# Where the Norms' second halves and block 2's gates stand in a two-block trunk kernel

## The chip, the cores and the metric

The kernel runs on one core of a Trainium2 chip. The metric is the device time of one execution in microseconds, the median of several runs. The core has five engines with an instruction queue each: TensorE (PE), VectorE (DVE), ScalarE (ACT), GpSimd (POOL) and SyncE (SP), which here issues the DMAs.

## The reference

Two blocks of two layers each are computed over 512 latent tokens (`x`) and 256 context tokens (`ctx`), all with 1024 features in float32. Every layer of block 1 is a mixer (layer 0 an mLSTM, layer 1 a windowed attention), then a feed-forward part; each has a Norm ahead of it, which scales a token by the reciprocal of its root mean square and then scales and shifts its features:

```python
u = _modulate(_rms_norm(h, norm_mix[i]), mod_l[0], mod_l[1])
h = h + mod_l[2] * y                      # y: the mixer's output product
h = h + mod_l[5] * _sq_relu_mlp(_modulate(_rms_norm(h, norm_ffn[i]), mod_l[3], mod_l[4]), ...)
```

A layer of block 2 has three branches over the same input, a gate for each, one output product and a LayerNorm:

```python
mixed = jnp.einsum('gts,bnsgc->bntgc', w_s, vn) + b_s.T[None, None, :, :, None]     # in sgu
m = (jax.nn.sigmoid(ga) * (ya @ p['w_br_attn']) + jax.nn.sigmoid(gg) * (yg @ p['w_br_gla'])
     + jax.nn.sigmoid(gs) * (ys @ p['w_br_sgu']))
x_new = layer_norm(DEEPNORM_ALPHA * x + gate[:, None, :] * (m @ p['w_out']), p['post_g'], p['post_b'])
```

`ya` comes from an attention, `yg` from a gated linear attention (gla, a scan over chunks of 64 tokens) and `ys` from a spatial gating unit (sgu): `mixed` is its spatial product, within chunks of 128 tokens. `ga`, `gg` and `gs` are 1024 features each of a product of the layer's input with weights. The last layer of a block needs the latent tokens alone.

## The kernel before, in words

Features lie on the 128 partitions, tokens along the free axis. A product in float32 accuracy is made of three: an operand is split in a high and a low part (`whi`, `wlo` of the weights, `uhl`, `ull` of latent and `uhc`, `ulc` of context activations), and high-high, high-low and low-high are summed in a PSUM bank. A block of 128 output features over a segment so takes 8 x 3 = 24 matmuls. Segments are `LAT` (512 latent tokens), `CTX` (256 context tokens) and `HALVES` (the latent tokens in two halves, `H0` and `H1`). Two banks (`acc`) go round among the products, in some stages more (`accx`); a bank is free again when DVE or ACT has read it.

`sweep` (L397) runs a product over blocks and segments. At the end of a stage its last `nt` blocks (`tail`; 3, with LayerNorm 4 or 5) are taken segment by segment, so that the next Norm can be formed for the first segment while the second's products run. This is in the hands of a `Norm` object (L1894; `LayerNorm`, L1935, in block 2) with four calls: `add` accumulates squares of the residual in DVE and ACT (`nac`, `nal`, in LayerNorm `nsl`, `nsc` too), `stat` sums them over the partitions by matmuls with `onesd` (`colsum`) and takes the power -1/2 on POOL (`rs`, in LayerNorm `rv`), `spread` brings the result to all partitions by a matmul with the identity into the bank `ns`, and `make` forms the 8 blocks of `uh`, `ul` with it: a DVE product `sc`, an ACT modulation `uh`, a DVE or POOL difference `ul`. There are six stage ends with a Norm: A the mLSTM's output product, B the first ffn's, C the windowed attention's, D the second ffn's, E and F the output products of block 2's two layers. F is the end of the kernel.

In `b_layer` (L1731), `gla` (L1421) runs in pools of its own and calls `fill` for work that PE does between the steps of its scan. A step works in levels (`gqt`, `gkq` on DVE in two buffers each, then the small products `P` and `sm`). `fill` issues the gates (24 blocks of 128 features, L1640, a bank is freed by ACT's tanh and the result stored by a DMA to `th`) and `sgu` (L1585). The spatial products of sgu stand in four groups; each group and segment takes a bank, which DVE frees with the product `sc<-acc,vecs,st`, and POOL multiplies the result with `us`. In layer 0 a gate covers `LAT` and `CTX`, in layer 1 `LAT` alone. After gla, `merge` loads the branches and the gates again.

The order within an engine is not the order of the code: a scheduler with a model of time chooses among the instructions whose inputs it takes for ready, and the order of the code gives the priority. Each engine then works its list in order. Names in listings carry numbers: `acc_21963` is one use of a bank.

Of the kernel before, what the change touches and what calls it, by code (L numbers as in the profile page):

```python
# [239 lines left out]
class Net:  # L240
# [156 lines left out]
    def sweep(self, items, x, segs, use, kt=8, head=None, tail=None, nm=None, nt=3):  # L397

        n = len(items)

        def group(js, segs, nm=None):
            w = [self.ws(*items[j], kt) for j in js]
            for i, s in enumerate(segs):
                for j, wj in zip(js, w):
                    use(j, s, self.fm(wj, [x(s)], kt)[0])
                    self.step()
                    if nm and i and j == js[0]:
                        nm.spread(segs[i - 1])  # L410
                if nm:
                    nm.stat(s)
                    if i:
                        nm.make(segs[i - 1])
            if nm:
                nm.spread(segs[-1])
                nm.make(segs[-1])

        a, b = 3 if head else 0, n - nt if tail else n
        if head:  # L420
            group(range(a), head)
        for j in range(a, b):
            group([j], segs)
        if tail:
            with self.weights("wt", nt) if nt > 3 else contextlib.nullcontext():
                group(range(b, n), tail, nm)
# [1155 lines left out]
                y = slice(t * P + 32 * b, t * P + 32 * b + 32)  # L1582
                self.mm(pS[t // 2][32 * b:32 * b + 32, t % 2, lev, :], k[:, y], q[:, y])

    def sgu(self, u, l, ph, d, between):  # L1585
        nc = self.nc
        full = l == 0
        us = self.t(ph, [P, 4, T if full else TL], "us")
        segs = [LAT, CTX][:1 + full]
        wT, bs, t2 = [self.t(ph, [P, 512], n) for n in ("swT", "sbs", "st2")]  # L1590
        nc.sync.dma_start(out=wT, in_=self.ins["swT"][l])
        nc.sync.dma_start(out=bs, in_=self.ins["sgu_b"][l].partition_broadcast(P))
        ps = self.acc()
        self.mm(ps, self.ones, wT)
        for g in range(4):
            x = slice(g * P, (g + 1) * P)
            self.stt(t2[:, x], ps[:, x], self.vec("sgu_ln_b_2", 1, l * 4 + g), bs[:, x], MULT, ADD)

        def items(n):
            return [((n, l, i), c) for i in range(2) for c in range(2)]  # L1600

        def up(f, s, ps):
            x = us[:, f, self.cols(s)]
            self.stt(x, x, 0.5, ps, MULT, MULT)

        self.sweep(items("b_sg"), lambda s: self.part(u, s), segs,
                   lambda f, s, ps: self.silu2(ps, us[:, f, self.cols(s)]))
        self.sweep(items("b_su"), lambda s: self.part(u, s), segs, up)
        chunks = range(6 if full else 4)
        sv = self.t(ph, [P, len(chunks), 512], "sv")  # L1610
        for i in range(2):
            w = self.wt(("b_sv", l, i))
            for c in chunks:
                ps = self.acc(256)
                self.tmm(ps, self.uchunk(u, c), w)
                (self.act if c % 2 else nc.vector.tensor_copy)(sv[:, c, i * 256:(i + 1) * 256], ps)
        for c in chunks:
            b6 = self.t(ph, [P, 6], "sb6", bufs=2)
            mv = self.t(ph, [P, 2], "smv", bufs=2)
            nc.vector.bn_stats(b6, sv[:, c, :])  # L1620
            nc.vector.bn_aggr(mv, b6)
            self.ts(mv[:, 1:2], mv[:, 1:2], EPS, ADD)
            self.tt(mv[:, 1:2], mv[:, 1:2], self.nhalf[:, 0:1], ALU.pow, eng=nc.gpsimd)
            self.ts(sv[:, c, :], sv[:, c, :], mv[:, 0:1], SUB, mv[:, 1:2], MULT)
        between()
        for g in range(4):
            x = slice(g * P, (g + 1) * P)
            for s in segs:
                y = self.cols(s)
                nt, c0 = s.n // P, y.start // P  # L1630
                ps = self.acc(s.n).rearrange("p (t x) -> p t x", x=P)
                for t in range(nt):
                    self.mm(ps[:, t, :], sv[:, c0 + t, x], wT[:, x])
                m = self.scr(s.n)
                self.stt(m.rearrange("p (t x) -> p t x", x=P), ps, self.vec("sgu_ln_g_2", 1, l * 4 + g),
                         t2[:, x].unsqueeze(1).to_broadcast([P, nt, P]), MULT, ADD)
                self.tt(us[:, g, y], m, us[:, g, y], MULT, eng=nc.gpsimd)
                nc.sync.dma_start(out=d["ys"][:, g, y], in_=us[:, g, y])

    def gates(self, u, l, d, items):  # L1640

# [89 lines left out]
    def b_layer(self, u, l, x_src, norm, x_dst, xd):  # L1731

        nc = self.nc
        segs = [s for s in ("l", "c") if s == "l" or l == 0]
        ntok = {"l": TL, "c": TC}
        tail = [LAT, CTX] if l == 0 else HALVES
        d = {n: self.t(xd, sh, f"{n}{l}") for n, sh in
             (("ya", [P, 4, T]), ("yg", [P, 4, T]), ("ys", [P, 4, T]), ("gg", [P, 4, T]), ("gv", [P, 6, 512]), ("gqk", [4, P, T]),  # L1740
              ("th", [24, P, T]))}
        g0 = 3 + l

        def fill():
            self.gla_in(u, l, d)
            self.gates(u, l, d, range(0, g0))

        self.b_attn(u, l, d["ya"], fill)
        if self.dbg_fn:
            self.dbg(f"ya{l}", d["ya"])  # L1750

        def fill():
            a, b = ((6, 9), (8, 10))[l]
            self.gates(u, l, d, range(g0, a))
            with self.pool("sg") as ph:
                self.sgu(u, l, ph, d, lambda: self.gates(u, l, d, range(a, b)))
            self.gates(u, l, d, range(b, 24))

        self.gla(u, l, d, fill)
        if self.dbg_fn:  # L1760
            self.dbg(f"yg{l}", d["yg"])
            self.dbg(f"ys{l}", d["ys"])
        def residual(ph):

            z = {s: self.t(ph, [P, KC, ntok[s]], "z" + s) for s in segs}
            rs, w = self.t(ph, [P, TL], "rs"), self.t(ph, [P, 2, 8], "wb")
            for s, r in norm[0]:
                ps = self.acc(s.n)
                self.spread(ps, r)
                self.act(rs[:, s.o:s.o + s.n], ps)  # L1770
            for i, v in enumerate(norm[1:]):
                if v is not None:
                    self.ts(w[:, i], v, ALPHA, MULT)
            for s in segs:
                nc.sync.dma_start(out=z[s], in_=x_src[s])
                for c in range(KC):
                    x = z[s][:, c, :]
                    if s == "c":
                        self.act(x, x, scale=ALPHA)
                        continue  # L1780
                    self.tt(x, x, rs, MULT, eng=nc.gpsimd)
                    if norm[2] is None:
                        self.act(x, x, scale=w[:, 0, c:c + 1])
                    else:
                        self.act(x, x, AF.Identity, scale=w[:, 0, c:c + 1], bias=w[:, 1, c:c + 1])
            return z

        with contextlib.ExitStack() as es:
            y, z = {}, None
            if l:  # L1790
                ph = es.enter_context(self.pool("ln", side="right"))
            with self.pool("mg") as pm, self.banks(6, 0):
                if l:
                    z = residual(ph)
                self.merge(pm, l, d, y)
            if not l:
                ph = es.enter_context(self.pool("ln", side="right"))
            with self.banks(2, 4):

                z = z or residual(ph)  # L1800
                gh = self.t(ph, [P, 8, 2], "gh")[:, :, :len(segs)]
                self.ts(gh, self.mod2[l][:, 16:24, :len(segs)], 0.5, MULT)
                un = {} if l == 0 else None
                nm = LayerNorm(self, ph, z, l, un, x_dst)
                self.proj_res([("b_wo", l, i) for i in range(4)], y, z, {s: gh[:, :, "lc".index(s)] for s in segs},
                              [LAT, CTX][:len(segs)], tail, nm, nt=5 - l)
        return un, [(s, nm.r[s][1]) for s in tail if s.kind == "l"]
# [222 lines left out]
```

## Time and profile before

| | |
|---|---|
| median of 3 runs | 3182.08 us (3178.27 to 3183.65) |
| the profiled execution | 3184.52 us, span 3182.7 us |
| granted clock of PE, mean | 0.987 |
| PE busy | 3073.9 us (97%) |
| DVE busy | 1811.0 us (57%) |
| ACT busy | 1315.4 us (41%) |
| POOL busy | 717.6 us (23%) |

The span runs from the first to the last instruction. The granted clock is PE's, as a share of 2.4 GHz; 0.5 is 1.2 GHz. The share of the chain that ended last is PE 83%, DVE 6%, time without a visible cause 4%, DMA 3%, ACT 2%. Times in the rows below are microseconds from the span's start.

### The profile page before, as it was taken

Reading aid. Unit: us, or ns where it says so; the run is one execution under the profiler, and the core shown is the slowest. Engines: PE = TensorE matmul, PEld = TensorE weight load, DVE = VectorE, ACT = ScalarE, POOL = GpSimd, SP = SyncE. Lnnn points to the kernel's source line nnn. Section 1 sums busy time; section 2 is a strip of 40 time slices with the busy share of each in tenths; the row PEclk is TensorE's granted clock in tenths of the full one; section 3 lists DMA queues with packets and bytes.
Section 4 is the critical chain, followed back from the end, with each engine's and each line's share of the span. In section 5 each row is a group of like instructions: output and inputs, shape, how many; then the busy total and the mean of one; then the engine's idle time right before and its main releaser. Section 6 shows DMA issues by size and latency. Waiting matters only on the chain.

```text
span 3182.7 us, 50932 instructions
## 1 busy us (share of the span) xinstructions
PE 3073.9 (97%) x19777; PEld 2568.4 (81%) x19777; DVE 1811.0 (57%) x3504; ACT 1315.4 (41%) x2661; POOL 717.6 (23%) x842
## 2 busy tenths in 40 slices
PE   7999999999999999999999999998999899999998
PEld 5778888888888955888889976787888789667788
DVE  4567667566755653633357420788524685158766
ACT  4344442213134575422245543544321456355443
POOL 1133121102021200211123000236213630013444
PEclk9999999999999999999999999999999999999999
DMA  6553324554431111322231222322544222233272
GB/s 242 180 173 97 110 87 161 163 176 142 159 100 59 49 42 45 126 95 98 93 119 51 74 74 86 97 83 82 190 130 158 79 67 85 94 121 110 94 248 80
DMA packets 149634, 359.52 MB, mean 113 GB/s; under 512 B 16049, under 2 KB 52689, under 8 KB 145297
## 3 DMA queue, kind: packets, MB, share of 16 engines
q1 hardware_dynamic: 149392, 356.27, 34.5%
q8 instruction: 155, 2.54, 0.3%
q14 instruction: 87, 0.70, 0.1%
HBM read 316.35 MB, written 39.71 MB: 112 GB/s over the span
## 4 chain that ended last, share of the span: by engine, by line
PE 83%; DVE 6%; issue 4%; DMA 3%; ACT 2%; POOL 1%; SPq 0%; ACTq 0%; DVEq 0%; POOLq 0%
PE acc L294 44%; PE accx L294 23%; PE s L294 4%; PE o L294 3%; PE st L294 3%; PE ada L294 1%; PE num L294 1%; DMA k<-gqk 1%; PE st L298 1%; DVE gqt L290 1%; DVE wlo L278 1%; PE x L294 1%; DVE ggx L278 1%; DMA raw<-in_ws_dram 1%; DVE gst L290 1%
## 5 line engine op out<-in xcount | busy, mean ns | idle before, releaser
L274 ACT ACTIVATE whi<-raw 128x1024 fp32r<-128x1024 f32 (+1 forms) x339 | 356.0, 1052 | 567.2 <-PE acc L294 272.2
L278 DVE TENSOR_TENSOR wlo<-raw,whi 128x1024 fp32r<-128x1024 f32 (+1 forms) x315 | 402.6, 1280 | 304.6 <-ACT whi L274 289.1
L294 PE MATMUL acc<-uhl,whi 128*128 128x512 f32 (+2 forms) x1208 | 469.4, 389 | 6.9 <-DVE sc L290 2.6
L294 PE MATMUL acc<-ull,whi 128*128 128x512 f32 (+2 forms) x1208 | 466.7, 387 | 0.0
L294 PE MATMUL acc<-uhl,wlo 128*128 128x512 f32 (+2 forms) x1208 | 466.0, 386 | 0.0
L294 PEld LDWEIGHTS acc<-uhl,whi 128*128 128x128 f32 (+1 forms) x1208 | 229.0, 190 | 59.4 <-issue 3.2
L278 POOL TENSOR_TENSOR sc<-sc 128x512 f32<-128x512 f32 (+1 forms) x99 | 122.7, 1241 | 671.6 <-ACT sc L274 658.0
L294 PEld LDWEIGHTS acc<-uhl,wlo 128*128 128x128 f32 (+1 forms) x1208 | 228.6, 189 | 46.3 <-issue 1.1
L294 PEld LDWEIGHTS acc<-ull,whi 128*128 128x128 f32 (+1 forms) x1208 | 229.2, 190 | 43.8 <-issue 2.5
L294 PE MATMUL acc<-whi,uhl 128*128 128x256 f32 x736 | 213.7, 292 | 3.5 <-ACT whi L274 1.5
L294 PE MATMUL acc<-whi,ull 128*128 128x256 f32 x736 | 213.2, 290 | 0.9 <-POOL ull L278 0.5
L294 PE MATMUL acc<-wlo,uhl 128*128 128x256 f32 x736 | 211.8, 289 | 0.8 <-DVE wlo L278 0.8
L294 PE MATMUL accx<-uhl,whi 128*128 128x512 f32 (+2 forms) x544 | 197.8, 366 | 8.7 <-DVE zc L290 5.3
L290 DVE SCALAR_TENSOR_TENSOR aacc<-araw,cond,aacc 128x512 f32<-128x512 f32 x266 | 203.7, 799 | 3.6 <-DMA araw<-in_ws_dram 2.7
L294 PE MATMUL accx<-ull,whi 128*128 128x512 f32 (+2 forms) x544 | 198.8, 366 | 1.8 <-DVE ull L290 1.8
L294 PE MATMUL accx<-uhl,wlo 128*128 128x512 f32 (+2 forms) x544 | 197.8, 364 | 0.0
L294 PE MATMUL acc<-uhc,whi 128*128 128x256 f32 (+1 forms) x656 | 187.6, 286 | 2.2 <-ACT uhc L274 2.2
L1065 DVE TENSOR_REDUCE nm<-s 128x1 f32<-128x512 f32 (+2 forms) x184 | 118.7, 663 | 122.7 <-PE s L294 121.7
L294 PE MATMUL acc<-ulc,whi 128*128 128x256 f32 (+1 forms) x656 | 187.9, 286 | 0.0
L294 PE MATMUL acc<-uhc,wlo 128*128 128x256 f32 (+1 forms) x656 | 187.3, 285 | 0.0
L278 POOL TENSOR_TENSOR wlo<-raw,whi 128x1024 fp32r<-128x1024 f32 x24 | 58.0, 2418 | 463.1 <-ACT whi L274 450.5
L294 PE MATMUL accx<-al,whi 128*128 128x512 f32 (+1 forms) x464 | 162.4, 350 | 0.0
(488 smaller groups left out, 7624.0 us busy)
## 6 DMA issues: line engine op xcount, KB each, us to landing
raw<-in_ws_dram SPq DMA_DIRECT2D x336, 512.0 KB
araw<-in_ws_dram SPq DMA_DIRECT2D x192, 256.0 KB
ar<-in_ws_dram SPq DMA_DIRECT2D x24, 1024.0 KB
th<-sc SPq DMA_DIRECT2D x48, 256.0 KB
th<-th SPq DMA_DIRECT2D x24, 384.0 KB
mb<-mcd SPq DMA_DIRECT2D x48, 128.0 KB
cb<-mcd SPq DMA_DIRECT2D x48, 128.0 KB
th<-th SPq DMA_DIRECT2D x24, 256.0 KB
```

Of the source, the lines that this page charges most:

```text
L274: self.last = self.nc.scalar.activation(out, in_, f, **kw)
L278: r = (eng or self.nc.vector).tensor_tensor(out, a, b, op=op)
L290: self.lastv = self.nc.vector.scalar_tensor_tensor(out, a, s, b, op0=op0, op1=op1)
L294: return self.nc.tensor.matmul(ps, l, r, start=start, stop=stop)
L298: self.nc.tensor.transpose(ps, x, self.ident[:k, :k])
L1065: nc.vector.tensor_reduce(nm[:, e, h:h + k], ps, axis=AX.X, op=MIN)
```

## The change

In `sweep`, `nm.make(segs[i - 1])` is issued behind the second block (`js[1]`) of the next segment; it was issued after that segment's last block and after `nm.stat(s)`. In `b_layer`, the gates that stood behind `sgu` are taken from an iterator: two of them are issued after each of the spatial groups 0, 1 and 2, the rest up to 21 behind `sgu`, and gates 22 and 23 after `gla` has closed its pools. No instruction's shape changes.

```diff
@@ sweep, group
                     if nm and i and j == js[0]:
                         nm.spread(segs[i - 1])
+                    if nm and i and j == js[1]:
+                        nm.make(segs[i - 1])
                 if nm:
                     nm.stat(s)
-                    if i:
-                        nm.make(segs[i - 1])
             if nm:
                 nm.spread(segs[-1])
                 nm.make(segs[-1])
@@ sgu, the end of a group's loop
                 self.tt(us[:, g, y], m, us[:, g, y], MULT, eng=nc.gpsimd)
                 nc.sync.dma_start(out=d["ys"][:, g, y], in_=us[:, g, y])
+            if g < 3:
+                among()
@@ b_layer
         def fill():
             a, b = ((6, 9), (8, 10))[l]
+            items = iter(range(a, 22))
+
+            def some(n):
+                self.gates(u, l, d, list(itertools.islice(items, n)))
+
             self.gates(u, l, d, range(g0, a))
             with self.pool("sg") as ph:
-                self.sgu(u, l, ph, d, lambda: self.gates(u, l, d, range(a, b)))
-            self.gates(u, l, d, range(b, 24))
+                self.sgu(u, l, ph, d, lambda: some(b - a), lambda: some(2))
+            self.gates(u, l, d, list(items))
 
         self.gla(u, l, d, fill)
+        self.gates(u, l, d, range(22, 24))
```

What this does to the engines' lists is shown at three places. First PE at stage end A, before, among the products of the first segment (`accx`, over `uhl`); `ns_4584` with `k_ident` is the `spread` of the second segment:

```order
2130 L294 MATMUL accx_4708<-uhl_4594,whi_4690 128x512
2131 L294 MATMUL accx_4747<-uhl_4594,whi_4696 128x512
2132 L294 MATMUL accx_4789<-uhl_4594,whi_4702 128x512
2133 L294 MATMUL ns_4584<-k_ident_71,rs_4587 128x128 x2
2134 L294 MATMUL accx_4708<-ull_4595,whi_4690 128x512
2135 L294 MATMUL accx_4708<-uhl_4594,wlo_4691 128x512
2136 L294 MATMUL accx_4708<-uhl_4594,whi_4690 128x512
```

The same `spread` on PE in the changed kernel, where it is `ns_4626`:

```order
2180 L294 MATMUL accx_4789<-uhl_4559,wlo_4703 128x512
2181 L294 MATMUL accx_4789<-uhl_4559,whi_4702 128x512
2182 L294 MATMUL accx_4789<-ull_4560,whi_4702 128x512
2183 L294 MATMUL accx_4789<-uhl_4559,wlo_4703 128x512
2184 L294 MATMUL ns_4626<-k_ident_71,rs_4629 128x128 x2
2185 L294 MATMUL acc_4830<-uhc_4638,whi_4690 128x256
2186 L294 MATMUL acc_4869<-uhc_4638,whi_4696 128x256
2187 L294 MATMUL acc_4830<-ulc_4639,whi_4690 128x256
```

The `spread` moved from row 2133, with 52 products of the first segment behind it, to row 2184, where the second segment's products follow at once. Its `colsum` moved from row 2114 to row 2164.

Second, PE at the spatial products of layer 0 before, the last six of eight (`acc<-swT,sv`), and the first product of the gate behind them (`acc_21894`):

```order
11600 L294 MATMUL y_20097<-gst_19655,gqxc_19685 128x128
11601 L294 MATMUL y_20097<-gv_18719,gpm_20091 128x128
11602 L294 MATMUL y_20097<-gst_19655,gqxc_19685 128x128
11603 L294 MATMUL acc_21848<-swT_20767,sv_21258 128x128 x2
11604 L294 MATMUL acc_21855<-swT_20767,sv_21258 128x128 x4
11605 L294 MATMUL acc_21864<-swT_20767,sv_21258 128x128 x2
11606 L294 MATMUL acc_21871<-swT_20767,sv_21258 128x128 x4
11607 L294 MATMUL acc_21880<-swT_20767,sv_21258 128x128 x2
11608 L294 MATMUL acc_21894<-uhl_15470,whi_21888 128x512
11609 L294 MATMUL acc_21894<-ull_15471,whi_21888 128x512
```

PE in the changed kernel at the second of the four pairs, from the end of a gate (`acc_21935`) to the start of the next (`acc_21985`):

```order
11700 L294 MATMUL acc_21935<-ulc_15036,whi_21901 128x256
11701 L294 MATMUL acc_21935<-uhc_15035,wlo_21902 128x256
11702 L294 MATMUL acc_21963<-swT_20767,sv_21258 128x128 x2
11703 L294 MATMUL x_20197<-gv_18719,gkt_20195 128x128 x4
11704 L294 MATMUL P_20213<-gqt_20234,gkq_20235 64x64 x8
11705 L294 MATMUL acc_21963<-swT_20767,sv_21258 128x128 x2
11706 L294 MATMUL acc_21972<-swT_20767,sv_21258 128x128 x2
11707 L294 MATMUL P_20213<-gqt_20252,gkq_20253 32x32 x16
11708 L294 MATMUL sm_20214<-gqt_20278,gkq_20279 32x32 x8
11709 L294 MATMUL sm_20215<-gqt_20278,gkq_20279 32x32 x8
11710 L294 MATMUL acc_21985<-uhl_15435,whi_21979 128x512
```

The eight products stood close together before; now a pair stands between gates, at this place with the products of three levels of gla around it. The third pair (rows 11817 to 11829) has four levels of half the columns around it, the first and the fourth none.

Third, DVE in the changed kernel at the same place; `sc_21968` is the product that frees the bank of `acc_21963`:

```order
2207 L290 SCALAR_TENSOR_TENSOR gqt_20252<-q_3317_19649,rf_18652,gE_20248 128x16x16
2208 L290 SCALAR_TENSOR_TENSOR gkq_20253<-k_3318_19650,rf_18652,gE_20248 128x16x16
2209 L290 SCALAR_TENSOR_TENSOR gkq_20253<-k_3318_19650,rb_18653,gE_20248 128x16x16
2210 L290 SCALAR_TENSOR_TENSOR gqt_20278<-q_3317_19649,rb_18653,gE_20274 128x32x8
2211 L290 SCALAR_TENSOR_TENSOR gst_20116<-gst_20116,gdec_20118,gkv_20117 64x128 x2
2212 L290 SCALAR_TENSOR_TENSOR gqt_20278<-q_3317_19649,rf_18652,gE_20274 128x32x8
2213 L278 TENSOR_TENSOR gkq_20279<-k_3318_19650,gE_20274 128x512
2214 L290 SCALAR_TENSOR_TENSOR sc_21968<-acc_21963,vecs_77,st_3519_20769 128x512
2215 L290 SCALAR_TENSOR_TENSOR gst_20116<-gst_20116,gdec_20118,gkv_20117 64x128
2216 L290 SCALAR_TENSOR_TENSOR sc_21975<-acc_21972,vecs_77,st_3519_20769 128x256
```

DVE before, around the third pair there (`acc_21855`, `acc_21864`):

```order
2173 L278 TENSOR_TENSOR gqxc_20146<-gqxc_20146,q_3317_19649 128x256
2174 L278 TENSOR_TENSOR ggx_20167<-gzm_20162,gzl_20161 64x512
2175 L278 TENSOR_TENSOR ggx_20167<-gzm_20162,gzl_20161 64x4x127
2176 L290 SCALAR_TENSOR_TENSOR sc_21860<-acc_21855,vecs_77,st_3519_20769 128x512
2177 L287 TENSOR_SCALAR gms_20104<-gms_20104 128x2
2178 L290 SCALAR_TENSOR_TENSOR sc_21867<-acc_21864,vecs_77,st_3519_20769 128x256
```

The bank products moved from behind `ggx` to behind a level's `gqt` and `gkq`, at the second pair.

## Rows read from the trace of the kernel before

**Rows 1.** The page, part 1: busy time, share of the span, instructions.

```profile
PE 3073.9 (97%) x19777; PEld 2568.4 (81%) x19777; DVE 1811.0 (57%) x3504; ACT 1315.4 (41%) x2661; POOL 717.6 (23%) x842
```

**Rows 2.** PE's waits, whole run: us in total, times, longest.

```profile
PE acc L294 <- DVE sc L290: 11.6, 4, 4.2
...
PE ns L294 <- POOL rs L278: 4.0, 3, 1.5
...
PE ns L294 <- DVE nsc L278: 2.9, 1, 2.9
...
PE ns L294 <- DVE nac L278: 1.7, 3, 0.8
```

**Rows 3.** Timeline, PE, layer 0's spatial products: start, duration, idle before, releaser.

```profile
2207.24 2.93 PE L294 MATMUL acc<-swT,sv 128*128 128x128 f32 x12 [4.10 <-DVE sc L290]
```

**Rows 4.** Timeline, PE, layer 1's spatial products.

```profile
2938.96 3.78 PE L294 MATMUL acc<-swT,sv 128*128 128x128 f32 x16 [4.16 <-DVE sc L290]
```

**Rows 5.** Timeline, DVE, at the same place.

```profile
2204.48 1.92 DVE L278 TENSOR_TENSOR ggx<-gzm,gzl 64x512 f32<-64x512 f32 x2
2206.43 0.75 DVE L290 SCALAR_TENSOR_TENSOR sc<-acc,vecs,st 128x512 f32<-128x512 f32 x1
```

**Rows 6.** Windows: length, busy us of PE, PEld, DVE, ACT, POOL; granted clock.

```profile
2206.50:2216.80 10.30, 6.99 (x22) 5.87 (x23) 10.13 (x20) 2.68 (x6) 7.17 (x9) 0.50 0.22 79
2937.00:2943.80 6.80, 4.84 (x22) 4.84 (x23) 6.77 (x8) 4.70 (x10) 5.53 (x7) 0.50 0.57 186
...
2850.00:3037.00 187.00, 172.66 (x1651) 144.08 (x1652) 148.08 (x261) 91.24 (x140) 76.44 (x94) 0.95 0.31 100
2271.00:2350.00 79.00, 79.00 (x453) 69.70 (x451) 18.97 (x18) 26.76 (x40) 9.57 (x4) 1.00 0.60 204
```

**Rows 7.** Timeline, PE, stage end A.

```profile
436.19 0.58 PE L294 MATMUL ns<-k_onesd,nac 128*128 128x1 f32 x4 [0.50 <-DVE nac L278]
437.89 0.50 PE L294 MATMUL accx<-ull,whi 128*128 128x512 f32 x1 [1.13 <-DVE ull L290]
...
455.52 0.39 PE L294 MATMUL accx<-uhl,wlo 128*128 128x512 f32 x1
455.75 0.28 PE L294 MATMUL acc<-uhc,whi 128*128 128x256 f32 x1
455.87 0.28 PE L294 MATMUL acc<-ulc,whi 128*128 128x256 f32 x1
```

**Rows 8.** Timeline, all engines, layer 1, a level beside a POOL product.

```profile
2942.89 1.59 POOL L278 TENSOR_TENSOR us<-sc,us 128x512 f32<-128x512 f32 x1 [1.21 <-DVE sc L290]
...
2943.26 1.50 DVE L290 SCALAR_TENSOR_TENSOR gqt<-q,rb,gE 128x256 f32<-128x256 f32 x1
...
2944.69 0.47 DVE L290 SCALAR_TENSOR_TENSOR gqt<-q,rf,gE 128x256 f32<-128x256 f32 x1
```

**Rows 9.** Groups by line, DVE, 2850 to 3037: count, busy us, mean ns.

```profile
L290 DVE SCALAR_TENSOR_TENSOR gst<-gst,gdec,gkv 64x128 f32<-64x128 f32 x36 | 17.2, 478 | 1.2 <-POOL gst L1460 0.7
L290 DVE SCALAR_TENSOR_TENSOR gqt<-q,rb,gE 128x256 f32<-128x256 f32 x25 | 15.3, 611 | 2.1 <-PE sm L294 1.7 <-PE P L294 0.3
```

**Rows 10.** PE's waits in 2850 to 3037, layer 1's gla.

```profile
PE sm L294 <- DVE gkq L278: 5.2, 3, 1.9
```

**Rows 11.** Timeline, all engines, stage end A: the second segment's spread, uhc, ulc.

```profile
443.71 0.61 PE L294 MATMUL ns<-k_ident,rs 128*128 128x128 f32 x4
...
444.94 0.51 ACT L274 ACTIVATE uhc<-sc,mod 128x256 fp32r<-128x256 f32 x1 [1.11 <-DVE sc L290]
...
446.05 0.47 DVE L290 SCALAR_TENSOR_TENSOR ulc<-sc,mod,uhc 128x256 fp32r<-128x256 f32 x1
```

**Rows 12.** Timeline, PE, stage end D.

```profile
1658.12 0.61 PE L294 MATMUL ns<-k_onesd,nal 128*128 128x1 f32 x4 [1.69 <-DVE nal L278]
```

**Rows 13.** Timeline, PE, the kernel's end.

```profile
3171.84 0.58 PE L294 MATMUL ns<-k_onesd,nal 128*128 128x1 f32 x4
...
3173.83 1.22 PE L294 MATMUL ns<-k_ident,rv 128*128 128x128 f32 x4 [0.47 <-POOL rv L278]
```

More of the change, by code (lines that the diff above doesn't have):

```diff
@@ L1583, in small, with sgu @@
                 self.mm(pS[t // 2][32 * b:32 * b + 32, t % 2, lev, :], k[:, y], q[:, y])
-    def sgu(self, u, l, ph, d, between):
+    def sgu(self, u, l, ph, d, between, among):
         nc = self.nc
```

## The prediction

> **What bounds the kernel now.** I read the page's shares first [rows 1]: TensorE (PE) is busy for 3073.9 of 3182.7 us, 97% of the span. An edit that leaves PE's work alone, as this one does, can only win PE's idle time, 3182.7 - 3073.9 = 109 us over the run, and stretches at the lower clock. So the second view is the list of what PE waited for [rows 2]. Its entry `acc` after `sc` of VectorE (DVE), 11.6 us in four waits, is the wait of a spatial product or a gate for a PSUM bank that a DVE product has not read yet. The entries on `ns` are the statistics of the Norms: `colsum` waits for `nac`, `nal` or `nsc`, `spread` for `rs`. Third come timelines of these places, fourth the windows with the granted clock.
>
> At the spatial products of layer 0 PE has three of the four waits, the longest 4.10 us [rows 3]; with layer 1's one of 4.16 [rows 4] taken off, 11.6 - 4.2 = 7.4 us are layer 0's. DVE explains them [rows 5]: two `ggx` of gla (1.92 us) stand ahead of the product that frees the bank, and more of gla's work between the next ones. In the stretch 2206.5 to 2216.8 the granted clock was 0.50, the 1.2 GHz level, with PE busy for 6.99 us [rows 6]; that work takes half the time at 2.4 GHz, so 3.5 us were lost. Layer 1 lost half of 4.84, 2.4 us, in the same way [rows 6]. At most 7.4 + 3.5 + 4.2 + 2.4 = 17.5 us are to be had here.
>
> **Part two, the gates.** Nothing is added: gate products move to places behind spatial groups 0, 1 and 2. The full 17.5 us go only if PE has work all along. Two gates in layer 0 are 48 products of 512 columns, 0.23 us apart, and 48 of 256, 0.12 apart [rows 7]: 17 us of PE, far more than DVE needs to free a pair of banks. But the order shows what else moves in layer 0. Behind the second pair of spatial products PE has P and sm products of gla back to back with no gate between them; the first gate behind them needs the bank that DVE's product on `acc_21963` frees, and that stands behind `gqt_20278` and `gkq_20279`. These levels have two buffers, so DVE starts one when PE has read the level two before. A level is four DVE products of 0.47, at starts 0.40 apart [rows 8], 1.6 us. Two levels, three `gst` of 0.48 [rows 9] and the bank's product of 0.75 [rows 5] are 1.6 + 1.6 + 1.4 + 0.7 = 5.3 us of DVE behind PE's last gate, of which PE's own small products cover about 2 (an estimate): a new wait of 3.3. Behind the third pair stand levels with half the columns; two of them, at three quarters of 1.6, and the bank's product are 3.1, less 0.9 under PE's work: 2.2. So 5.5 come back, and 1.5 for the clock, between none and two stretches like layer 1's, 4.8. Layer 0: -7.4 - 3.5 + 5.5 + 1.5 = -3.9, with -10.9 and -0.6 as ends.
>
> Layer 1 has half the gate work (the latent segment alone). In 2850 to 3037 DVE is busy for 148 of 187 us [rows 6], and PE waits 5.2 us for `sm` levels [rows 10]. Gates that go early are missing later as cover for these. I give half of the 6.6 back: -3.3, ends -6.6 and 0.
>
> The two gates behind the pools (22 and 23) cost nothing in layer 0: PE was busy for all of 2271 to 2350, gates alone [rows 6]. In layer 1 they are the last gates in either order. SP issues the merge's loads of `ya`, `yg` and `ys` from that place; some 11 us of gates cover them, and if that cover goes the merge starts late by a load, a few us at most.
>
> **Part one, the Norms.** At the kernel's end (the last LayerNorm) the order is the same: 0. At the five other stage ends `make` of the first segment gets ahead of `stat` of the second. As `spread` of the first stands where it stood, its `make` begins no earlier; what moves is `colsum` and `spread` of the second segment, to the end of the first one's products.
>
> Stage end A (block 1's first Norm): the wait of 0.50 for `colsum` goes, and of the 1.13 behind it [rows 7] the 0.4 that DVE spends on `nac` ahead of `ull` (an estimate by the 256-column products of [rows 8]): -0.9. Before, `spread` at 443.71 had 52 products behind it, and the second segment's `make` ran under them: its first `uhc` product at 455.75 waits for nothing [rows 7]. Now `spread` stands directly ahead of the products that need it. From its start to the end of the first `uhc` is 443.71 to 445.45, 1.7 us, less 0.3 of its own work: 1.4 of idle [rows 11]. The first `ulc` ended 1.1 later, at 446.52, which I count as 0.7, as an `ull` stood in between. After that `make` gives a 128-row block each 0.74 (two DVE products at 0.40 and the switches), and two product blocks use one in six starts of 0.12, 0.72: no more wait. A: -0.9 + 1.4 + 0.7 = +1.2, ends -1.6 (0.50 + 1.13 gone, all else hidden) and +3.
>
> B (end of the first ffn): the longest wait for `nac`, 0.8, and the longest for `rs`, 1.5 [rows 2], go. In their place `colsum` waits for a `nac` that now follows the whole first `make`: about 2.0, an estimate from A, where `make` gives its blocks at 0.74 and B's products of 256 columns use them at 0.72 from a first wait on. And `spread` stands 9 products of 0.12 ahead of its group, which leaves 1.0 of A's 1.4 + 0.7. B: +0.7, ends -2.3 and +4. C (swa's end): as A with shorter products, +1.2, ends -0.7 and +3.
>
> D (end of the second ffn): the wait of 1.69 [rows 12] and one for `rs`, 4.0 - 1.5 - 1.5 = 1.0 [rows 2], go. `colsum` is now followed at once by `spread`, a chain that took 3171.84 to 3173.83, 2.0 us, at the kernel's end [rows 13]: -0.7, ends -2.7 and +1.7 (a `colsum` that waits as before). E (layer 0's LayerNorm): the 2.9 for `nsc` [rows 2] go from the head, but the stage ends with the chain through the second segment's `make` and the attention weights' casts behind it, and this starts as late as before: +0.3, ends -2.9 and +1. Part one: +1.2 + 0.7 + 1.2 - 0.7 + 0.3 = +2.7, ends -10.2 and +12.7.
>
> **Sum.** -3.9 - 3.3 + 2.7 = -4.5 us. Against the profiled execution's own 3184.5 us that is 3180.0; that execution lies 2.4 above the median of the runs, 3182.1, so the forecast for the median is 3177.6, in round numbers 3178.
>
> **Rivals.** First, the levels of gla find cover (DVE runs ahead under the 17 us of gates per pair): the whole 17.5 go, with part one at +2.7 that is -14.8, 3167. For it speaks that a pair of gates is three times the 5.3 us of DVE; against it the two buffers of each level.
>
> Second, a wash: gla is paced by DVE in both layers, and what PE gains among the spatial products it waits later on the same chain, before the merge. +2.7, 3185. For it speaks DVE's share in layer 1 [rows 6]; against it that layer 0 has 79 us of gates left behind gla.
>
> Third, stage ends A, B and C at their dear ends, the second `make` being exposed: 3 + 4 + 3 - 0.7 + 0.3 = +9.6, with -7.2 that is +2.4; with D and E dear too, +5.5, 3188.
>
> Fourth, on the other side: GpSimd (POOL) slows DVE where PE now has no cover. The rows show it happen: `gqt` took 1.50 us beside POOL's `us` product of 1.59, and 0.47 just behind it [rows 8]. Each spatial product is followed by such a POOL product. Before, they fell into a stretch in which PE waited for banks anyway; now three pairs in layer 0 and three products in layer 1 stand next to levels that PE waits for. Nine times 1.03 is 9.3 us, and the waits of layer 0 then bring the lower clock in full, 4.8 for 1.5: -10.9 + 5.5 + 4.8 - 3.3 + 9.3 + 2.7 = +8.1, 3190. It ends above 0.2% from about seven such meetings on. The `gqt` products of layer 1 average 0.61 [rows 9], so few met a POOL product there before.
>
> The Trainium skill gives the cause a rule in its GPSIMD Engine Reference, Key points: GpSimd shares its SBUF interfaces with VectorE and contends with instructions that have two SBUF inputs. By that rule each level product next to a POOL product is slowed and this fourth case comes; the trace agrees where the two overlapped, 1.50 for 0.47.
>
> **Numbers.** Chances: forecast 0.42, full gain 0.23, wash 0.12, dear stage ends 0.12, slowed DVE 0.11. This kernel's measurement can tell 0.2%, 6.4 us, from no change. Faster by more than that takes the full gain and a third of the forecast's case, whose own range is 3171 to 3184: 0.23 + 0.14 = 0.37. Slower takes the last case and half of the dear stage ends: 0.17. The rest, 0.46, is within. The range runs from the full gain to the slowed DVE: 3166 to 3190.
>
> **What would show it.** Right: the four waits on `acc` after `sc` are gone, with both stretches at 0.50 there, and in layer 0 two waits of 2 to 3 us stand at `sm` or at the gate behind it. At A and C the second segment's first `uhc` or `uhl` products wait 1.5 to 2.5 us where they waited for nothing, and `colsum` at the head waits no more. Wrong: no new waits at the levels (full gain), as much more idle time ahead of layer 1's merge as was won (wash), a mean of `gqt` above 0.7 in either layer (slowed DVE), or A to E together outside -2 to +8.

## The result, and the profile after

The changed kernel took 3200.75 us (median of 4 runs, 3194.98 to 3201.03) against 3182.86 us of the kernel before: ratio 1.0058, 95% interval 1.0045 to 1.0071. It is 18 us slower. The forecast was 3178, the range 3166 to 3190.

The page after, part 1, answers to [rows 1]. The instructions are the same, yet PE is busy 9 us longer:

```profile
PE 3083.0 (96%) x19777; PEld 2575.0 (80%) x19777; DVE 1814.4 (57%) x3504; ACT 1312.6 (41%) x2661; POOL 710.6 (22%) x842
```

Where the time went is read from windows between the same matmuls, counted on PE, in both traces. The columns are those of [rows 6]: length, busy time of PE first, granted clock ahead of the DMA's share. Before, the stage ends A to E, then the stretches of gla and sgu in layers 0 and 1:

```profile
419.60:546.70 127.10, 123.84 (x701) 104.04 (x700) 95.89 (x143) 45.55 (x76) 24.93 (x24) 0.99 0.39 129
992.50:1071.20 78.70, 74.53 (x601) 72.70 (x600) 51.75 (x133) 39.83 (x92) 20.30 (x26) 1.00 0.16 53
1281.60:1350.20 68.60, 66.14 (x402) 58.85 (x401) 45.72 (x74) 33.25 (x63) 20.23 (x19) 0.98 0.41 131
1655.70:1713.50 57.80, 52.47 (x402) 51.03 (x401) 48.48 (x142) 33.86 (x91) 29.13 (x36) 0.91 0.31 99
2193.80:2320.00 126.20, 118.75 (x1021) 103.75 (x1010) 69.57 (x118) 49.94 (x82) 46.95 (x61) 0.96 0.47 160
2460.00:2735.30 275.30, 261.28 (x1601) 232.80 (x1600) 166.94 (x313) 140.17 (x329) 87.17 (x79) 0.98 0.26 88
2909.40:3123.50 214.10, 200.22 (x1426) 167.77 (x1414) 150.33 (x222) 91.46 (x134) 97.64 (x93) 0.96 0.50 165
```

The same in the changed kernel (A, B, C, D, layer 0's gla, E, layer 1's gla):

```profile
420.50:553.00 132.50, 127.01 (x702) 105.76 (x702) 97.45 (x141) 44.00 (x76) 25.80 (x24) 0.97 0.37 124
998.70:1084.40 85.70, 78.81 (x602) 76.77 (x601) 51.56 (x133) 39.71 (x92) 20.17 (x26) 0.94 0.15 48
1294.80:1366.80 72.00, 67.69 (x403) 60.02 (x401) 48.45 (x74) 33.02 (x63) 18.00 (x19) 0.95 0.38 124
1672.20:1735.70 63.50, 53.38 (x402) 52.20 (x401) 48.49 (x142) 34.04 (x91) 28.49 (x36) 0.89 0.27 90
2214.80:2340.70 125.90, 119.27 (x1020) 103.98 (x1007) 69.55 (x118) 49.83 (x82) 45.91 (x61) 0.96 0.46 160
2480.70:2760.30 279.60, 263.36 (x1602) 233.08 (x1601) 166.33 (x312) 141.58 (x331) 85.66 (x79) 0.97 0.25 85
2933.40:3139.90 206.50, 195.37 (x1424) 164.70 (x1411) 150.13 (x222) 90.97 (x134) 97.27 (x93) 0.98 0.51 171
```

The lengths differ by +5.4, +7.0, +3.4 and +5.7 at A to D and +4.3 at E: part one costs 25.8 us. Layer 0's gates give 0.3, layer 1's 7.6. These seven stretches are 17.9 us longer in sum and the whole span 16.1; the other 1.8 lie in parts that the change does not touch. Length less busy time is PE's idle time: at the five stage ends it grew by 13.8 us, and the same matmuls were busy 12.0 us longer, at a granted clock that is lower in each of the windows. These are two executions, and others of the same order scatter. In e2 below, which has part one alone with the same order at A to E, the idle time grew by 13.5 us and the busy time by 8.6, so the idle time is the steadier part. Layer 1's stretch took 214.1, 212.2, 210.7, 211.8 and 212.2 us in five executions of the order of before (before, e2, e3, e6, e8) and 206.5, 206.1, 205.7 and 206.9 in four of the changed one (after, e1, e4, e16): 5.9 us between the medians, so nearly 2 of the 7.6 are scatter.

At A the waits of `colsum` (0.50) and of the first `ull` (1.13) in [rows 7] became one of 2.20 for `ull`, and the second segment's first products now wait. PE's timeline after:

```profile
438.82 0.50 PE L294 MATMUL accx<-ull,whi 128*128 128x512 f32 x1 [2.20 <-DVE ull L290]
458.50 0.50 PE L294 MATMUL acc<-uhc,whi 128*128 128x256 f32 x2 [1.17 <-ACT uhc L274]
459.53 0.45 PE L294 MATMUL acc<-ulc,whi 128*128 128x256 f32 x1 [0.53 <-DVE ulc L290]
```

At B `colsum` waits 2.47 us behind the whole first `make`, where it waited 0.8 ([rows 2], `nac`). PE after:

```profile
1025.97 0.72 PE L294 MATMUL ns<-k_onesd,nac 128*128 128x1 f32 x4 [2.47 <-DVE den L1090]
```

DVE shows why. The last addition to the second segment's sum, `nac`, stood behind two products of `make`, first line; in the changed kernel it stands behind all of them (the releaser `den` is a short memset right behind it):

```profile
1008.86 0.42 DVE L278 TENSOR_TENSOR nac<-nac,sc 128x256 f32<-128x256 f32 x1
```

```profile
1025.17 0.74 DVE L278 TENSOR_TENSOR nac<-nac,sc 128x256 f32<-128x256 f32 x1 [0.42 <-ACT sc L274]
1025.87 0.07 DVE L1090 MEMSET den<- 128x8 f32 x1
```

At D the wait of 1.69 for `nal` [rows 12] is gone, but the next instruction waits longer for its weights (3.70, before 1.50), and `spread` waits 4.04 for `rs`. PE, then POOL:

```profile
1676.66 0.39 PE L294 MATMUL acc<-whi,uhl 128*128 128x256 f32 x1 [3.70 <-ACT whi L274]
...
1686.68 1.22 PE L294 MATMUL ns<-k_ident,rs 128*128 128x128 f32 x4 [4.04 <-POOL rs L278]
1689.08 0.58 PE L294 MATMUL acc<-whi,uhl 128*128 128x256 f32 x1 [1.17 <-ACT uhl L274]
```

```profile
1680.45 5.41 POOL L1049 MEMSET q<- 2x1024 f32 x6
1685.93 0.70 POOL L278 TENSOR_TENSOR rs<-rs,nhalf 128x2 f32<-128x2 f32 x1
```

Before, the same step from `colsum` (1658.12, [rows 12]) to `spread` took even longer, 7.3 us, but products stood between the two, and only 0.95 was left as a wait for `rs`:

```profile
1665.39 1.23 PE L294 MATMUL ns<-k_ident,rs 128*128 128x128 f32 x4 [0.95 <-POOL rs L278]
```

In layer 0 the waits for DVE's bank products, 0.75, 4.10 [rows 3] and 2.57, are down to one of 0.80, and the levels wait instead: 3.29 us at the place that the prediction named, behind the second pair. A spatial product ahead of it waits 1.21 for ACT. Behind the third pair stand 0.60 and 0.53 at `sm` and the 0.80 at the gate.

```profile
2242.48 0.71 PE L294 MATMUL acc<-swT,sv 128*128 128x128 f32 x4 [1.21 <-ACT sc L274]
2246.87 0.66 PE L294 MATMUL sm<-gqt,gkq 128*32 128x32 f32 x32 [3.29 <-DVE gkq L278]
```

In layer 1 the wait of 4.16 [rows 4] is still there, now on the first gate. What went are later waits. First the changed kernel, then the one before:

```profile
2962.18 0.79 PE L294 MATMUL acc<-uhl,whi 128*128 128x512 f32 x1 [4.17 <-DVE sc L290]
2982.57 0.79 PE L294 MATMUL acc<-uhl,whi 128*128 128x512 f32 x1 [2.15 <-ACT sc L274]
```

```profile
2961.18 0.46 PE L294 MATMUL sm<-gqt,gkq 128*32 128x32 f32 x32 [1.32 <-DVE gkq L278]
2963.57 0.46 PE L294 MATMUL sm<-gqt,gkq 128*32 128x32 f32 x32 [1.93 <-DVE gkq L278]
2965.32 0.66 PE L298 MATMUL x<-k_ident,gkx 128*128 128x128 f32 x2 [1.29 <-DVE gkx L278]
```

### The profile page after: what moved, and what is told of

It reads as the page before. It is cut to its first block, busy times and chain, and to the rows that moved or that the text cites. A ratio compares the mean times of both kernels' runs of the same rounds, so it can differ in the third digit from the quotient of the medians.

```text
span 3198.8 us, 50932 instructions
## 1 busy us (share of the span) xinstructions
PE 3083.0 (96%) x19777; PEld 2575.0 (80%) x19777; DVE 1814.4 (57%) x3504; ACT 1312.6 (41%) x2661; POOL 710.6 (22%) x842
## 5 line engine op out<-in xcount | busy, mean ns | idle before, releaser
L294 PE MATMUL accx<-ah,wlo 128*128 128x512 f32 (+1 forms) x464 | 162.4, 351 | 0.0
L294 PE MATMUL accx<-ah,whi 128*128 128x512 f32 (+1 forms) x464 | 162.4, 351 | 0.0
```

Source lines behind the costliest of these rows:

```text
L294: return self.nc.tensor.matmul(ps, l, r, start=start, stop=stop)
```

## The experiments

**The two parts apart.** e1 is the change without its edit in `sweep`, e2 that edit alone:

```diff
 # e2, in sweep
+                    if nm and i and j == js[1]:
+                        nm.make(segs[i - 1])
                 if nm:
                     nm.stat(s)
-                    if i:
-                        nm.make(segs[i - 1])
```

> The gates as in the change, the Norms as before. By the reading that the two parts do separate things (theory S), this keeps the 7.6 us that layer 1's gla stretch won in the profile after and the 0.3 of layer 0's, and none of the 25.5 that the five stage ends lost: 3182.9 - 8 = 3175 us, ratio 0.997 to 0.998. By the rival that the gain in layer 1 only came because the Norms' loss had shifted the work ahead of it (theory I, the parts act on each other): 3183 within 3 us, ratio 1.000.

> The Norms as in the change, the gates as before. Theory S: the five stage ends lose what they lost in the profile after, 5.3, 7.0, 3.3, 5.6 and 4.3 us, 25.5 in all: 3208 us, ratio 1.008. Theory I: the parts' effects do not add, the time is at or under the changed kernel's 3201, ratio 1.004 to 1.006.

Measured: e1 3176.3 us, ratio 0.9980 (0.9972 to 0.9989); e2 3202.5, ratio 1.0061 (1.0047 to 1.0074). By its ratio e2 lies nearer to theory I's 1.006 than to theory S's 1.008; the places decide. In e1 the stage ends A to E are within 0.3 us of before, and layer 1's stretch is 206.1 us. In e2 they are +3.8, +5.9, +2.2, +5.7 and +4.5, and layer 1's stretch is 212.2. So each part acts at its own places, and the loss is part one's. e2 came out 5 us under the expected 3208: the kernel before took 3180.4 beside it and not 3182.9, and A, B and C are 1.1 to 1.6 us shorter than in the changed kernel at the same order and nearly the same idle time, with less time at the lower clock.

**What in part one costs.** Two orders of the code between before and the change:

```diff
 # e3: behind the last block's use, ahead of stat
                 if nm:
+                    if i:
+                        nm.make(segs[i - 1])
                     nm.stat(s)
-                    if i:
-                        nm.make(segs[i - 1])
```

```diff
 # e6: behind the last block's product, ahead of its use
-                    use(j, s, self.fm(wj, [x(s)], kt)[0])
+                    ps = self.fm(wj, [x(s)], kt)[0]
+                    if nm and i and j == js[-1]:
+                        nm.make(segs[i - 1])
+                    use(j, s, ps)
```

> Gates as before. make of the first segment is issued behind the last block of the second segment, as before, but ahead of stat of the second segment. If what costs is that make overtakes stat (its DVE and ACT products stand ahead of the second segment's sums, theory O), the stage ends lose as in the change: 3200 to 3210 us. If what costs is the earlier place, behind the second block, by which the third block's residual and squares fall behind make as well (theory P): close to the kernel before, 3183 to 3188.

> Gates as before. make of the first segment is issued behind the third block's product but ahead of that block's use (its residual product and the square and sum for the Norm). Theory P1 (the loss is that the third block's use, which the second segment's sums need, falls behind make on DVE and ACT): as slow as the change's Norms, 3198 to 3206, stage ends A to E together +18 to +26. Rival P2 (the loss is that make competes from the second block on with the products themselves and the weights' splits): close to before, 3181 to 3188.

Measured: e3 3180.3, ratio 1.0001 (0.9991 to 1.0011); e6 3199.9, ratio 1.0056 (1.0043 to 1.0068). In e6 A to E are +3.8, +5.8, +2.2, +5.7 and +2.6.

The lists of the engines say what this shows. In e3 the scheduler left every list as it was: PE, DVE, ACT and POOL work the same instructions in the same order as before. Nothing overtook anything on the chip, so e3 does not test theory O; it is the kernel before once more. In e6 the lists at A to D are those of e2. So it is enough for the loss at A to D that `make` comes ahead of the last block's `use`, the residual product and the square and sum on ACT and DVE that `colsum` needs. DVE's `nac` at B, above, is the addition that comes late there: with `make` ahead of it, the second segment's sum is complete only when the first segment's blocks are formed. At D the rival P2 has a share that no run takes apart: the 3.70 us are a wait for a weight's high part `whi`, which ACT splits behind `make`'s modulations.

**D's wait for `rs`.** e7 is e2 with the memsets of L1049 on VectorE (`self.nc.vector.memset` for `self.nc.gpsimd.memset`):

> The Norms as in the change, gates as before, and the memsets of q2's two rows on VectorE in place of GpSimd. If stage end D's wait of 4.0 us for rs is GpSimd's queue of memsets of 0.94 us ahead of the power (theory M), that wait falls to 2 us or less, stage D loses 3 us or more of its 63.5, and B's tail likewise; the whole 3196 to 3200. If rs waits for its colsum's own chain (rival), the wait stays at 3.5 to 4 and the time at 3202.

Measured: 3201.9, ratio 1.0056 (1.0041 to 1.0072), e2's time. PE at D:

```profile
1684.42 0.71 PE L294 MATMUL ns<-k_ident,rs 128*128 128x128 f32 x4 [1.13 <-POOL rs L278]
1689.66 0.58 PE L294 MATMUL acc<-whi,uhl 128*128 128x256 f32 x1 [4.53 <-ACT uhl L274]
```

The wait for `rs` did fall from 3.83 in e2 to 1.13, so POOL's memsets made most of it. But the next wait grew from 1.17 to 4.53: DVE now runs the memsets ahead of `make`, and D took 64.0 us, not 3 less than 63.5. The expected time was wrong, since it let one wait go without asking what is late next.

**The lower clock.** e13 is e2 with matmuls that nobody reads in that wait of D:

```diff
 # shortened: the loop stands in a helper, with a count of 12 at D and 0 elsewhere
+                ps = self.nbank()[:, :s.n]
+                for k in range(12):
+                    self.mm(ps, nm.cut(nm.acc, s)[:, :P], nm.cut(nm.x, s)[:, k % KC])
                 nm.spread(segs[-1])
```

> The Norms as in the change, gates as before, and at stage end D twelve matmuls that nobody reads between colsum and spread, where PE waits 3.8 us for rs. They take time in which PE had nothing to do. Theory C (the lower clock behind the wait comes from PE's idling, and is 3 of the stage's 5.7 us): the stretch at 0.50 from some 1681 to 1692 ends early or goes, D falls from 63.5 to 60 to 62 us, the whole 3199 to 3201. Rival (the clock falls there whatever PE does, or the other waits of D bring it): D stays at 63.5 or grows by what the matmuls take beyond the wait.

Measured: 3194.7, ratio 1.0039 (1.0026 to 1.0053). 21 us from just ahead of `colsum` on, first e2, then e13:

```profile
1677.00:1698.00 21.00, 15.55 (x98) 14.88 (x97) 11.53 (x33) 6.65 (x20) 9.33 (x14) 0.73 0.21 70
```

```profile
1675.00:1696.00 21.00, 19.18 (x124) 18.18 (x124) 11.26 (x33) 7.08 (x23) 9.90 (x14) 0.90 0.20 66
```

With the wait filled the mean clock of these 21 us is 0.90 against 0.73. Over all of D it is 0.95, against 0.87 to 0.89 in three executions of the same order without the filling (after, e2, e6). So here the clock falls, at least in part, because PE idles. D itself gains next to nothing (63.2 us for 63.5), as the rival had it, because the filling, 5.3 us, is longer than the wait. The other 7 us between e2 and e13 do not come from D. Behind the added instructions the scheduler set its lists anew for some 1100 us, in 3784 of PE's 19777 places. Layer 0's stretch is 118.8 us in e13, 126.0 in e2, but what stands ahead of it in block 2 is 3.0 longer.

**Which gates win.** e4 has the change's gates in layer 1 alone, e14 three per group there, e8 only gates 22 and 23 behind the pools, in both layers:

```diff
 # e4; e14 has 3 * l, e8 no gates among the groups
+                self.sgu(u, l, ph, d, lambda: some(b - a), lambda: some(2 * l))
```

> The gates as in the change in layer 1 alone; layer 0's gates and all Norms as before. If layer 0 gains nothing because its new waits at the sm levels and the lower clock took back what the bank waits gave (profile after: 126.2 before, 125.9 after), this is as fast as the gates in both layers: 3175 us, ratio 0.9975. If layer 0's part had a gain that the profile does not show, this is slower than the gates in both layers by 2 us or more: 3177 to 3180.

> Norms as before; of the gates' change only the two last gates (22, 23) are issued behind gla's pools, in both layers; none among the spatial groups. Theory G (layer 1's gain of 8 us comes from the gates among the spatial groups, which cover the sm levels behind them): as before, 3180 within 2.5. Rival (it comes from the two gates held back for the end of gla): 3174 to 3177, with layer 1's stretch near 206 us.

> As the gates of layer 1 alone, with three gates behind each of the groups 0, 1 and 2 in place of two. If cover for the sm levels is what counts and the late levels have enough left, 3173 to 3175; if the later levels then lack cover (a P wait of 2.5 and an sm wait of 1.2 already stand there), 3176 to 3179.

Measured: e4 3175.5, ratio 0.9979 (0.9971 to 0.9988); e8 3180.8, 0.9995 (0.9986 to 1.0004); e14 3174.4, 0.9977 (0.9967 to 0.9986). Layer 1's gates alone are as fast as both layers', holding back the two last gates does nothing by itself, three per group are as good as two.

**A version with the memsets moved.** e10 is e4 with them on VectorE:

> The faster version tried: layer 1's gates among the spatial groups, all else as before, and q2's memsets on VectorE. Before, stage ends B and D wait 1.5 and 1.0 us for rs behind GpSimd's memsets; with these gone and the lower clock of D shortened, 3170 to 3174 against 3175.5 of the gates alone. If VectorE, which holds the second segment's make there, has no room for eight memsets, it is no faster or slower: 3175 to 3178.

Measured: 3184.2, ratio 1.0004 (0.9995 to 1.0013): it loses what e4 won. D is 63.7 us long in place of e4's 57.9; VectorE had no room.

**Layer 0.** e11 (the change's gates) and e12 (the kernel before), both without the small levels' key products there:

```diff
-                                self.tt(kt, k_, E, MULT)
+                                if full:
+                                    kt = k_
+                                else:
+                                    self.tt(kt, k_, E, MULT)
```

> Gates as in the change, Norms as before; left out: in layer 0 the decayed key of the four small levels (VectorE's product gkq of 512 columns; the plain key is used). Theory L (layer 0's new wait of 3.3 us at the sm levels is VectorE's time for a level behind two buffers): the wait falls by 0.7 to 1.5 us and layer 0's stretch is shorter than the control's by 2 us or more. Rival (the level waits for its decay from GpSimd and ACT, not for VectorE's products): the wait stays within 0.4 of 3.3.

> The control: the kernel before with the same products left out in layer 0. The bank waits of 0.75, 4.10 and 2.57 us at the spatial products stay within 1.5 us in sum, since gla's ggx and gst stand ahead of the bank products there; layer 0's stretch 124 to 126.2 us.

One execution each: layer 0's stretch is 129.9 us in e11 and 133.9 in e12. The difference of 4 is in the expected sense, and the wait of 3.3 is gone, but a wait of 2.25 at `P` stands in its place, and the control did not stay at 126: its order changed too, with a wait of 3.62 at `P`. This pair settles nothing. The next moves the place instead: e15 is e14, e16 is e1, both with layer 0's sgu one gate earlier.

```diff
-            a, b = ((6, 9), (8, 10))[l]
+            a, b = ((5, 8), (8, 10))[l]
```

> Three gates among the groups in layer 1 as in the run before it, and in layer 0 no gates among the groups, but sgu starts one gate earlier (gates up to 5 ahead of it, up to 8 ahead of the spatial products, in place of 6 and 9). In DVE's list the eight bank products then stand together with short products of gla between, where ggx, gst and the scans stood. Theory D (layer 0's waits for banks are set by which of gla's DVE work the bank products happen to stand behind, not by missing gates): the 7.4 us of waits fall under 2, layer 0's stretch from 126 to 117 to 120, the whole 3166 to 3170. Rival (the waits come from eight products on two banks in a row, wherever they stand): 3174 as without the shift.

> As the gates alone (the change's gates in both layers, Norms as before), with layer 0's sgu one gate earlier. At this place no levels of gla stand back to back around a spatial pair. Theory D: the sm waits of 3.3 us behind the second pair go, layer 0's stretch is 117 to 120, the whole 3168 to 3171. Rival (gates among the groups cost layer 0 new waits at any place): the stretch stays at 124 or more, the whole 3174 to 3177.

Measured: e15 3171.8, ratio 0.9970 (0.9959 to 0.9981), the lowest here, though not apart from e14's interval; e16 3177.3, 0.9986 (0.9978 to 0.9995). PE's waits from 1700 to 2290 in e15:

```profile
PE sm L294 <- DVE gkq L278: 6.0, 5, 2.6
PE x L298 <- DVE gkx L278: 4.0, 2, 2.4
PE acc L294 <- DVE us L290: 2.0, 3, 1.0
PE P L294 <- DVE gkq L290: 1.7, 2, 1.1
...
PE acc L294 <- DVE sc L290: 0.6, 1, 0.6
```

and before:

```profile
PE acc L294 <- DVE sc L290: 7.4, 3, 4.1
PE x L298 <- DVE gkx L278: 4.4, 2, 3.0
```

The waits for DVE's bank products fall from 7.4 to 0.6 with no gate among the groups: their place in gla's DVE work makes them. e13, whose new order also has no gates there, shows the same, 0.6 for e2's 7.5. But the other waits on gla's levels grow by as much. From the start of block 2 to layer 0's merge PE idles 18.4 us before, 16.8 in e1, 17.1 in e15, 19.2 in e16 and 16.7 in e13. That part takes 606.5, 605.7, 604.0, 606.4 and 600.5 us. Six other executions whose lists there are those of before (e2, e3, e4, e6, e8, e14) take 604.9 to 608.1 us with 16.8 to 19.3 idle, so neither e15 nor e16 shows a gain there that stands clear of this scatter, and none near the expected 7 us. Counted on the same matmuls layer 0's stretch is 125.1 us in e15 and 128.8 in e16, not 117 to 120. Only e13 is clearly shorter, and by its clock, with as much idle time. Neither theory holds as it was put. That gla is bound by DVE in layer 0 too would explain idle time that only moves; no run took enough of DVE's work away cleanly to show it.

## Why the prediction was wrong

- **Part one, +2.7: measured +25.8.** The order was read rightly: `spread` ahead of its group costs a wait (A's 1.17 + 0.53 for the 1.4 + 0.7 put down), `colsum` at B waits 2.47 for the 2.0. The step that failed first is the list of prices, which has no term for the clock at the stage ends, though A before already had a stretch at 0.50 behind three waits of 0.5 to 1.6. That is 12.0 of the 25.8 us here, 8.6 of 22.1 in e2. I had priced it only in part two. That stretch, from the kernel before:

```profile
438.40:441.80 3.40, 3.40 (x9) 2.65 (x9) 3.40 (x7) 2.70 (x4) 1.20 (x1) 0.50 0.04 12
```

- **Waits said to go that came back.** "A: -0.9" at the head was +0.6: `ull` waits 2.20. "D: the wait of 1.69 goes" was +2.2 on the next instruction, whose weights wait for ACT. "A chain of 2.0" at D was 4.04, because POOL has 5.4 us of memsets ahead of `rs`, as it had before; the price was taken from the kernel's end, where POOL's queue is empty. E's 2.9 went, and 2.48 and 1.41 came. Idle time at the stage ends so grew by 13.8, not 2.7. That is just above the 12.7 of all five dear ends.
- **Why the second sums are late.** The prediction put it to `make` getting ahead of `stat`, and priced a late addition (`nac`) at B alone. The trace at B and e6 show that the last block's `use` is what falls behind `make`. What overtaking `stat` alone would cost stays open, since e3's lists are those of before.
- **Layer 0, -3.9: measured -0.3.** The returning waits were right in place and nearly in size: 3.29 us for 3.3 behind the second pair and 1.93 for 2.2 behind the third; the 1.21 for ACT, which it did not name, makes 6.4 in all for 5.5. The clock's share was not: the stretches at 0.50 moved with the waits, 10.3 us long before and 10.2 after, and PE's busy time is 0.5 higher than before, where 2.0 less was counted.
- **Layer 1, -3.3: measured -7.6**, and -5.9 between the medians of several executions. The mechanism was wrong, and the right sign is luck. The 4.16 us did not go; the gates cover three later waits at `sm` and `x` (4.5 us before, one of 2.15 after), and the stretches at the lower clock there went from 17.0 us in all to 6.8, 4.9 us of PE's busy time in these two executions.
- **Gates 22 and 23, 0:** right (e8). The kernel's end: right in that its order is the same.
- **The rivals.** The case that came is the third, dear stage ends, at twice its price; its dear ends had no clock either. POOL's slowing of DVE did not come as a mean above 0.7: `gqt` averages 0.60 to 0.63 us in layer 1 after, 0.61 before [rows 9]. The full gain and the wash did not come either.

## What to carry to other kernels

When work is moved ahead of something, ask first what the next reduction still needs: here the loss came with the order in which forming one segment overtook the last addition to the other segment's sum. On a kernel that keeps PE 97% busy, price every new wait twice, once as idle time and once as the slower matmuls behind it, and look into the queue of each engine on the way (POOL's memsets) before taking a chain's time from an empty one. Where a scheduler orders the work, measure the parts of a change apart: here one part lost some 20 us and hid another's gain of 4 to 6. And compare the engines' lists before reading a result: an edit that leaves every list as it was tests nothing, and an edit at one place can set them anew far behind it.

## What the runs showed of the hardware that was not expected

The lower clock does not come at each execution of the same order: stage end C took 68.6 us before and 67.1 in e3, whose lists are the same, with 2.46 us of idle time in both; the granted clock over it was 0.98 in the one and 1.00 in the other. A memset of two partitions by 1024 elements takes nearly the same on either engine, 0.94 us on POOL and 0.91 on DVE.
